# Attention values and turned probabilities as two float32r parts each: three products in place of one float32 product

## The chip, the cores and the metric

The kernel runs on one core of one Trainium2 chip, in one launch. The metric is the device time of the launch in microseconds (us), the median over the runs shown. A profiled execution gives one trace, with its own time; the words for the engines are PE (TensorE, matrix products), PEld (its weight loads), DVE (VectorE), ACT (ScalarE), POOL (GpSimd) and SP (SyncE, which here issues the transfers of the weights).

## The reference, cut to what matters

Two layers over 256 tokens of width 1024. Each layer is half a SwiGLU block, a mixer, and half a SwiGLU block. The mixer of layer 0 is a convolution module, that of layer 1 is multi-head latent attention with 8 heads. Only the attention is touched here:

```python
def mla(h, positions, w_a, g_q, g_kv, w_uq, w_ukv, w_o):
    ...
    kv = jnp.einsum("bsc,chd->bshd", c_kv, w_ukv)
    k_nope, v = kv[..., :QK_NOPE], kv[..., QK_NOPE:]
    ...
    for blk in range(seq // Q_BLOCK):
        q0, q1 = blk * Q_BLOCK, (blk + 1) * Q_BLOCK
        s = (q_nope . k_nope + q_rope . k_rope) * scale
        s = jnp.where(mask[None, None], s, -jnp.inf)
        p = jax.nn.softmax(s, axis=-1).astype(v.dtype)
        outs.append(jnp.einsum("bhqk,bkhd->bqhd", p, v[:, :q1]))
    o = jnp.concatenate(outs, axis=1)
    return o.reshape(o.shape[0], seq, N_HEADS * V_HEAD) @ w_o
```

(the two products of `s` are written short here). Blocks of 128 queries see 128 and 256 keys, so that a head has three 128 by 128 tiles of probabilities.

## The kernel before, in words

**Weights.** Every weight comes from memory as a float32 block of 1 MB (`raw`, three buffers, issued by SP). `load` (L161) splits it into two float32r parts: ACT copies it to `hi` (L187), which rounds it, and DVE subtracts to get `lo` (L188); both in two pieces of 128x1024. There are five buffers of `hi` and `lo`. `casts` keeps the two instructions of each piece, so that later code can place them. A product of two such split operands is `mm3` (L271): three matmuls, high times low (L273), high times high (L276) and low times high (L277).

**Placing.** A scheduler lays out each engine's order from the program's order, priorities and a simulated timeline. `urgent` (L193) gives a function's instructions high priority and remembers the last one on each engine; `behind` puts the two casts of a later block after the last six remembered ones on their engine. `order(a, b)` puts `a` after `b` on one engine without a semaphore. Each engine then runs its own instructions strictly in the order laid out.

**PSUM.** Eight banks in three groups (`bank`): four of "A" (products), three of "B" (scores and turned tiles), one of "C" (here: the values of a head, `pv`).

**The attention stage**, from `mla_in`: queries and keys are made per head (`nope`, L1240 copies them out), and the values `VV` are made for all heads as four products of 512 columns, each copied from its bank by ACT (L1287). Then, for each head:

1. `scores`: float32 products of queries and keys into a bank "B" (L1299, L1300).
2. `softmax`, urgent: DVE takes the maxima (L1312) and scales them (L1313), ACT takes the powers and their sums (L1315), DVE the reciprocal (L1318) and the scaling (L1320), into `pr`.
3. `probs`: PE turns the three tiles of `pr` into a bank "B" (L317), and ACT copies them to `ptT` in float32 (L1327).
4. `values`: two float32 products into the one bank "C", 256 columns with the first 128 keys (L1336) and 128 columns with the second (L1337).
5. `evicted`: ACT casts the bank to `Oh` (L1331) and DVE subtracts to `Ol` (L1332). The next head's `values` can write the bank when both have read it. This is urgent for heads 3 to 6 only.

The output product `o` (`Rows`, with the four blocks of `w_o`, here wo[0] to wo[3]) adds head after head in four banks "A", by `mm3`. The loop at the end of `mla_in` writes heads in a staggered order: `scores(i)`, `probs(i - 2)`, `values(i - 3)`, with blocks of `o` and further weight loads between. Ahead of it stand four manual placements of the `lo` casts of wo[0] and wo[1] behind steps of the softmax of heads 0 to 2.

Of the kernel before, what the change touches and what calls it, by code (L numbers as in the profile page):

```python
# [11 lines left out]
F32 = mybir.dt.float32  # L12
F32R = mybir.dt.float32r
# [6 lines left out]
P = 128  # L20
D = 1024
S = 256
NT = S // P
# [8 lines left out]
H = 8  # L32
NOPE = 128
ROPE = 64
VH = 128
# [49 lines left out]
def trunk(ctx: ExitStack, tc: tile.TileContext, x, xt, first, pos, invf, gfin, wdw,  # L85
          f1w13, f1w2, f2w13, f2w2, cw1, cw2, wa, wuq, wukv, wo, wpair, out):
    nc = tc.nc
# [12 lines left out]
    def uid(s):  # L100
        n_uid[0] += 1
        return f"{s}_{n_uid[0]}"
# [4 lines left out]
    def bank(tag, name):  # L107
        return ps.tile([P, 512], F32, tag=tag, name=uid(name), bufs=BANKS[tag])
# [24 lines left out]
    n_used = [0]  # L133
# [3 lines left out]
    def order(ins, first):  # L137
        tc.add_manual_dep(ins.ins, first.name, mybir.DependencyInfo(
            mybir.DependencyClass.NoSync, mybir.DependencyReason.DATA), reason="order")
# [7 lines left out]
    casts = {}  # L147
# [45 lines left out]
    def urgent(f):  # L193

        def g(*args, **kw):
            traced = nc.cur_bb.bb.instructions
            n = len(traced)
            with tc.high_priority():
                r = f(*args, **kw)
            last = {ins.engine: ins for ins in traced[n:]}  # L200
            for engine, ins in last.items():
                ahead_of.setdefault(engine, []).append(ins)
            return r
        return g

    def load_ahead(ahead=W_BUFS - 2):
        load_to(min(len(blocks), n_used[0] + ahead))

    def load_to(last):
        while len(loaded) < last:  # L210
            loaded.append(load(blocks[len(loaded)], PIECES))

    def weights(n=1, more=True):
        out = []
        for _ in range(n):
            n_used[0] += 1
            if more:
                load_ahead()
            else:
                load_ahead(0)  # L220
            out.append(loaded[n_used[0] - 1])
        return out
# [19 lines left out]
    for k in range(KT):  # L242
        c = slice(k % 4 * 512, k % 4 * 512 + 512)
# [27 lines left out]
    def mm3(o, ah, al, bh, bl, start, stop, after=()):  # L271

        mm = nc.tensor.matmul(o, ah, bl, start=start, stop=False)  # L273
        for a in after:
            order(mm, a.ins)
        nc.tensor.matmul(o, ah, bh, start=False, stop=False)  # L276
        return nc.tensor.matmul(o, al, bh, start=False, stop=stop)  # L277
# [8 lines left out]
    def tbs(tb):  # L286
        return slice(tb * P, (tb + 1) * P)
# [26 lines left out]
    def transposed(src, q, n, after=(), turned=None):  # L314
        b = bank("B", "tp")
        for j in range(n):
            tp = nc.tensor.transpose(b[:, j * P:(j + 1) * P], src[:, (q + j) * P:(q + j + 1) * P], ident)  # L317
            if turned is not None:
                turned.append(tp)
            for a in after:  # L320
                order(tp, a.ins)
        return b
# [815 lines left out]
    def mla(X, make_next, cc, sn):  # L1138
        with tc.tile_pool(name="mla", bufs=1) as act:
            return mla_in(act, X, make_next, cc, sn)  # L1140

    def mla_in(act, X, make_next, cc, sn):
# [9 lines left out]
        for x, fill in ((KR, -1e30), (QR, 1.0)):  # L1152
            nc.gpsimd.memset(x, 0.0)
            for parity in range(2):
                for tb in range(NT):
                    row = 64 * (1 - parity) + 32 * tb
                    t = tb * P + (CHUNK if x is KR else 0)
# [67 lines left out]

        KN = xp.tile([P, H, S], F32, tag="Xh", name="KN")
        QN = xp.tile([P, H, S], F32, tag="Xl", name="QN")
        VV = act.tile([P, NT, H * VH], F32, tag="VV", name="VV")

        def nope(part, dst, nk, ch, cl, width, h0, heads, after=()):  # L1230

# [13 lines left out]
        qr, qu, lows, turned = [], [], [], []  # L1245
# [22 lines left out]
        for t in range(NT):  # L1268
            b = transposed(kd[t], 0, 1, (last,))
# [3 lines left out]
        for tb in range(NT):  # L1273
            b = transposed(qr[tb], 0, 4, (last,)).rearrange("p (j t) -> p j t", t=P)
# [6 lines left out]
        for tb in range(NT):  # L1281
            for d in range(2):
                b = bank("A", "v")
                for k in range(2):
                    c = slice(k * D + d * 512, k * D + d * 512 + 512)
                    mm3(b, CKh[:, k, tbs(tb)], CKl[:, k, tbs(tb)], hi[:, c], lo[:, c], k == 0, k == 1)
                kept = nc.scalar.copy(VV[:, tb, d * 512:(d + 1) * 512], b)  # L1287

        Oh = act.tile([P, H, S], F32R, tag="Oh", name="Oh")
        Ol = act.tile([P, H, S], F32R, tag="CQ", name="Ol")  # L1290

        score_last, maxima, powers, scaled = [], [], [], []

        def scores(hd):
            b = bank("B", "sc")
            sc = {0: b[:, :P], 1: b[:, P:P + S]}
            for qb in range(NT):
                n = (qb + 1) * P
                nc.tensor.matmul(sc[qb], QN[:, hd, tbs(qb)], KN[:, hd, :n], start=True, stop=False)  # L1299
                last = nc.tensor.matmul(sc[qb], QR[:, hd % 2, hd // 2, tbs(qb)], KR[:, hd % 2, :n], start=False,  # L1300
                                        stop=True)
            score_last.append(last)
            return softmax(sc)
# [19 lines left out]

        def probs(pr):
            b = transposed(pr, 0, 3)
            pt = act.tile([P, 3 * P], F32, tag="ptT", name=uid("ptT"), bufs=2)
            nc.scalar.copy(pt, b[:, :3 * P])  # L1327
            return pt

        def evicted(hd, b):  # L1330
            nc.scalar.copy(Oh[:, hd, :], b[:, :S])  # L1331
# [1 line left out]

        def values(hd, pt):
            b = bank("C", "pv")
            nc.tensor.matmul(b[:, :S], VV[:, 0, hd * VH:(hd + 1) * VH], pt[:, :S], start=True, stop=False)  # L1336
            nc.tensor.matmul(b[:, P:S], VV[:, 1, hd * VH:(hd + 1) * VH], pt[:, S:], start=False, stop=True)  # L1337

            (urgent if hd in (3, 4, 5, 6) else lambda f: f)(evicted)(hd, b)

        pr, pt = {}, {}
        part, = weights(1, False)
        load_ahead(1)

        table = urgent(nc.scalar.activation)(small.tile([P, 1], F32, tag="silu", name="exp"), neghalf, AF.Exp)
        order(table, kept.ins)
# [1 line left out]
        pr[1] = scores(1)  # L1348
        pr[2] = scores(2)

        for j, i, highs, lows in ((0, 0, None, maxima[2]), (0, 1, None, scaled[0]), (1, 0, powers[2], scaled[1]),
                                  (1, 1, powers[2], scaled[2])):
            for cast, first in zip(casts[n_used[0] + j, i], (highs, lows)):
                if first is not None:
                    order(cast, first.ins)
        nope(part, QN, 4, CQh, CQl, 512, 4, (0, 4), score_last[-1:])
        o = Rows(Oh, Ol, H)
        for i in range(2, H + 3):
            if 2 < i < H:
                pr[i] = scores(i)  # L1360
            if i == 6:
                load_ahead(5)
            if i in (3, 4):
                load_ahead(i - 1 + (i == 4))
            if i - 2 < H:
                pt[i - 2] = probs(pr[i - 2])
            if i - 3 in pt:
                values(i - 3, pt[i - 3])
            if i in (6, 8):
                o.block((i - 6) // 2)  # L1370

            if i in (8, 9):
                load_to(n_used[0] + i - 4)
# [39 lines left out]
    rows = ctx.enter_context(tc.tile_pool(name="rows", bufs=1))  # L1413
# [101 lines left out]
```

## Time and profile before

| | us |
|---|---|
| median of 3 runs | 919.18 |
| lowest and highest run | 918.69, 919.48 |
| the profiled execution, its own time | 918.68 |
| span of its trace | 916.9 |

The profiled execution lies 0.50 us below the median; 1.8 us of its time lie outside the span. Of the span, the attention stage from the making of the values to the last product of `w_o` that waits for a head takes the stretch from about 677 to 727 us. In the timeline view a row is one instruction, or several in succession by the same line on the same tiles: its start in us from the span's start, the time to the end of the last one, engine, line, operation, output and inputs, shape, and how many. A pair in square brackets is idle time of the engine before it, with what ended it. The ends of PE rows are modelled, since matmuls are pipelined: what one costs in a stream is read from start to start.

### The profile page before, as it was taken

The numbers are of one execution on the slowest core, as the hardware profiler recorded it, in microseconds if no ns is written. First come the engines' busy times: TensorE is split into PE (matmuls) and PEld (weight loads), VectorE is DVE, ScalarE is ACT, GpSimd is POOL, SyncE is SP. The second block draws the span as 40 slices with busy tenths as digits, with TensorE's granted clock in tenths as the row PEclk, the third lists the DMA queues.
The fourth block names the chain that finished last, engine by engine and source line by source line (L and its number), as shares of the span: only waits on it lengthen the run. The fifth ranks groups of instructions, "written<-read, shape, count | busy, mean of one in ns | idle before, by whom it ended". The sixth has DMA issues, their size and how long they took to land.

```text
span 916.9 us, 12085 instructions
## 1 busy us (share of the span) xinstructions
PE 908.9 (99%) x4337; PEld 764.6 (83%) x4337; DVE 591.1 (64%) x931; ACT 492.8 (54%) x842; POOL 127.6 (14%) x261
## 2 busy tenths in 40 slices
PE   9999999999999999999999999999999999999997
PEld 7888888898988888888888888888898888888886
DVE  6886764489987666655476665545768676566533
ACT  7654454388877444543364544443677574454422
POOL 1720000079951000000010000001400000000000
PEclk9999999999999999999999999999999999999999
DMA  9987776533227667766567777754445478776711
GB/s 339 321 294 248 277 253 222 188 139 138 93 85 270 243 233 239 251 222 226 184 203 271 260 244 239 239 203 132 168 143 184 149 258 277 250 250 217 252 46 46
DMA packets 65292, 194.73 MB, mean 212 GB/s; under 512 B 11728, under 2 KB 37200, under 8 KB 45904
## 3 DMA queue, kind: packets, MB, share of 16 engines
q1 hardware_dynamic: 64800, 193.28, 60.7%
q8 instruction: 34, 0.56, 0.2%
q10 hardware_dynamic: 432, 0.69, 0.2%
q14 instruction: 26, 0.21, 0.1%
HBM read 179.78 MB, written 14.16 MB: 212 GB/s over the span
## 4 chain that ended last, share of the span: by engine, by line
PE 99%; DMA 0%; ACT 0%; POOLq 0%; DVE 0%; issue 0%; POOL 0%; ACTq 0%
PE u L277 17%; PE u L273 17%; PE u L276 17%; PE o L273 10%; PE o L277 10%; PE o L276 10%; PE u L753 3%; PE gate L753 3%; PE o L988 2%; PE tp L317 1%; PE u L282 1%; PE pairs L796 1%; PE a L273 1%; PE a L277 1%; PE a L276 1%; PE nope L277 1%
## 5 line engine op out<-in xcount | busy, mean ns | idle before, releaser
L188 DVE TENSOR_TENSOR lo<-raw,hi 128x1024 fp32r<-128x1024 f32 (+1 forms) x292 | 344.8, 1220 | 175.9 <-ACT hi L187 174.8
L187 ACT CAST hi<-raw 128x1024 fp32r<-128x1024 f32 x294 | 292.6, 1047 | 240.8 <-PE o L277 85.5
L273 PE MATMUL u<-lo,Xh 128*128 128x512 f32 x688 | 268.0, 389 | 0.0
L276 PE MATMUL u<-hi,Xh 128*128 128x512 f32 x688 | 267.7, 389 | 0.0
L277 PE MATMUL u<-hi,Xl 128*128 128x512 f32 x688 | 267.6, 389 | 0.0
L277 PEld LDWEIGHTS u<-hi,Xl 128*128 128x128 f32 x688 | 129.1, 188 | 27.2 <-DVE Xl L336 0.5
L273 PEld LDWEIGHTS u<-lo,Xh 128*128 128x128 f32 x688 | 129.1, 188 | 27.0 <-DVE lo L188 0.4
L276 PEld LDWEIGHTS u<-hi,Xh 128*128 128x128 f32 x688 | 129.1, 188 | 27.0
L276 PE MATMUL o<-hi,Gh 128*128 128x512 f32 (+1 forms) x356 | 137.9, 387 | 0.0
L277 PE MATMUL o<-hi,Gl 128*128 128x512 f32 (+1 forms) x356 | 137.8, 387 | 0.0
L273 PE MATMUL o<-lo,Gh 128*128 128x512 f32 (+1 forms) x356 | 137.2, 387 | 0.0
L308 POOL TENSOR_TENSOR ms<-ss 128x1 f32<-128x1 f32 x16 | 10.0, 628 | 586.7 <-ACT junk L300 586.7
L277 PEld LDWEIGHTS o<-hi,Gl 128*128 128x128 f32 x356 | 66.9, 188 | 13.5
L273 PEld LDWEIGHTS o<-lo,Gh 128*128 128x128 f32 x356 | 66.9, 188 | 13.5
L276 PEld LDWEIGHTS o<-hi,Gh 128*128 128x128 f32 x356 | 66.9, 188 | 13.4
L640 DVE TENSOR_TENSOR Gl<-gb,Gh 128x512 fp32r<-128x512 f32 (+1 forms) x48 | 31.3, 652 | 56.6 <-ACT Gh L639 56.6
L639 ACT CAST Gh<-gb 128x512 fp32r<-128x512 f32 (+1 forms) x48 | 28.0, 583 | 73.3 <-DMA gb<-gd 73.3
L842 DVE SCALAR_TENSOR_TENSOR acc<-V,dw,acc 128x128 f32<-128x128 f32 (+1 forms) x174 | 53.9, 394 | 0.0
L863 ACT ACTIVATE prod<-V,dw 128x128 f32<-128x128 f32 (+1 forms) x128 | 45.6, 415 | 1.9 <-POOL Y L864 1.0
L715 DVE TENSOR_TENSOR s<-s,u 128x512 f32<-128x512 f32 (+1 forms) x48 | 30.5, 635 | 7.6 <-PE u L277 7.3
L714 ACT ACTIVATE s<-u,R 128x512 f32<-128x512 f32 (+1 forms) x48 | 31.2, 649 | 5.9 <-PE u L277 4.8
L864 POOL TENSOR_TENSOR odd<-odd,prod 128x128 f32<-128x128 f32 (+1 forms) x62 | 33.0, 536 | 0.2
(218 smaller groups left out, 858.1 us busy)
## 6 DMA issues: line engine op xcount, KB each, us to landing
raw<-in_f2w SPq DMA_DIRECT2D x66, 1024.0 KB, 4.9
raw<-in_f1w SPq DMA_DIRECT2D x62, 1024.0 KB, 5.0
raw<-in_cw SPq DMA_DIRECT2D x12, 1024.0 KB, 4.8
gd<-gt SPq DMA_DIRECT2D x160, 64.0 KB, 3.3
gb<-gd SPq DMA_DIRECT2D x40, 256.0 KB, 4.9
raw<-in_wo SPq DMA_DIRECT2D x4, 1024.0 KB, 4.8
raw<-in_wuq SPq DMA_DIRECT2D x3, 1024.0 KB, 4.8
raw<-in_f1w SPq DMA_DIRECT2D x8, 256.0 KB, 4.9
```

The source lines that it names most:

```text
L187: casts[len(loaded), i] = (nc.scalar.copy(hi[:, c], raw[:, c]), low.tensor_sub(lo[:, c], raw[:, c], hi[:, c].bitcast(F32)))
L188: low.tensor_sub(lo[:, c], raw[:, c], hi[:, c].bitcast(F32)))
L273: mm = nc.tensor.matmul(o, ah, bl, start=start, stop=False)
L276: nc.tensor.matmul(o, ah, bh, start=False, stop=False)
L277: return nc.tensor.matmul(o, al, bh, start=False, stop=stop)
L640: nc.vector.tensor_sub(Gl[:, f, tbs(tb)].rearrange("p t (i q) -> p t i q", q=32), bv, gh.bitcast(F32))
L714: nc.scalar.activation(s[:, :w], u[0, tb][:, :w], AF.Silu, scale=X.r[tb])
L715: nc.vector.tensor_mul(s[:, :w], s[:, :w], u[0, tb][:, w:] if both else u[1, tb])
L753: mm = nc.tensor.matmul(u[:, t], w[:, c], X.x[:, k, t], start=(k == 0), stop=(k == KT - 1))
L842: dve_last.append(nc.vector.scalar_tensor_tensor(out if j == j1 - 1 else y, v, w, y, op0=ALU.mult, op1=ALU.add))
L863: prods_last.append(nc.scalar.activation(p, v, AF.Copy, scale=w))
L864: pool_last.append(nc.gpsimd.tensor_tensor(o, o, p, op=ALU.add))
```

## The change

Values and turned probabilities become float32r pairs, and each of the two float32 products of a head becomes three float32r ones by `mm3`. That takes a second part of each operand, made by a subtraction on DVE: four `VL` of 128x512 for the values, and one `ptL` of 128x384 for each head. `VL` uses the buffers "hb" and "ht" of a pool that serves the normalisations on either side of the attention, `ptL` the three buffers "rp512" of the rotary step. Both subtractions are urgent. The two placements of wo[1]'s `lo` casts behind the softmax of heads 1 and 2 go; instead, they are put behind the `ptL` subtractions of heads 1 and 2.

```diff
-        VV = act.tile([P, NT, H * VH], F32, tag="VV", name="VV")
+
+        VV = act.tile([P, NT, H * VH], F32R, tag="VV", name="VV")
+        VL = {}
...
-                kept = nc.scalar.copy(VV[:, tb, d * 512:(d + 1) * 512], b)
+                vh = VV[:, tb, d * 512:(d + 1) * 512]
+                kept = nc.scalar.copy(vh, b)
+                VL[tb, d] = rows.tile([P, 512], F32R, tag=("hb", "ht")[d], name=uid("VL"), bufs=2)
+                urgent(nc.vector.tensor_sub)(VL[tb, d], b, vh.bitcast(F32))
...
+        turned_low = []
...
-            pt = act.tile([P, 3 * P], F32, tag="ptT", name=uid("ptT"), bufs=2)
+            pt = act.tile([P, 3 * P], F32R, tag="ptT", name=uid("ptT"), bufs=2)
             nc.scalar.copy(pt, b[:, :3 * P])
-            return pt
+            pl = act.tile([P, 512], F32R, tag="rp512", name=uid("ptL"), bufs=3)
+            turned_low.append(urgent(nc.vector.tensor_sub)(pl[:, :3 * P], b[:, :3 * P], pt.bitcast(F32)))
+            return pt, pl
...
-            nc.tensor.matmul(b[:, :S], VV[:, 0, hd * VH:(hd + 1) * VH], pt[:, :S], start=True, stop=False)
-            nc.tensor.matmul(b[:, P:S], VV[:, 1, hd * VH:(hd + 1) * VH], pt[:, S:], start=False, stop=True)
+            ph, pl = pt
+            c = slice(hd % 4 * VH, hd % 4 * VH + VH)
+            for tb, o, t in ((0, b[:, :S], slice(0, S)), (1, b[:, P:S], slice(S, S + P))):
+                mm3(o, VV[:, tb, hd * VH:(hd + 1) * VH], VL[tb, hd // 4][:, c], ph[:, t], pl[:, t], tb == 0, tb == 1)
...
+        n_part = n_used[0]
...
-        for j, i, highs, lows in ((0, 0, None, maxima[2]), (0, 1, None, scaled[0]), (1, 0, powers[2], scaled[1]),
-                                  (1, 1, powers[2], scaled[2])):
+        for j, i, highs, lows in ((0, 0, None, maxima[2]), (0, 1, None, scaled[0]), (1, 0, powers[2], None),
+                                  (1, 1, powers[2], None)):
...
                 pt[i - 2] = probs(pr[i - 2])
+                if i in (3, 4):
+                    order(casts[n_part + 1, i - 3][1], turned_low[-1].ins)
```

## The prediction

> **What bounds the kernel now.** I read the page first: its head, the granted clock, and the chain of work that ended last.
>
> ```profile
> span 916.9 us, 12085 instructions
> ...
> PE 908.9 (99%) x4337; PEld 764.6 (83%) x4337; DVE 591.1 (64%) x931; ACT 492.8 (54%) x842; POOL 127.6 (14%) x261
> ...
> PEclk9999999999999999999999999999999999999999
> ...
> PE 99%; DMA 0%; ACT 0%; POOLq 0%; DVE 0%; issue 0%; POOL 0%; ACTq 0%
> ```
>
> PE is the chain: 99% of it, with nine tenths of the full clock or more in every slice. So each ns of PE work in the attention stage is a ns of the end, in both directions, and a wait of PE that does not exist today is added whole. The second view is the list of PE's waits over the whole span.
>
> ```profile
> PE warm L265 <- DVE still L260: 1.0, 1, 1.0
> PE u L282 <- ACT Xh L457: 0.4, 1, 0.4
> ```
>
> Both belong to the start of the kernel. The trace has no wait of PE in the attention stage that a better order could give back, save a hint of 0.1 us that I come to below. A gain can therefore come only from cheaper products.
>
> **The products of a head.** The third view is PE's timeline where a head's values stand between long products of the output, and, for the price of split products, two neighbours in the queries' stage.
>
> ```profile
> 718.00 0.39 PE L276 MATMUL o<-hi,Oh 128*128 128x512 f32 x1
> 718.23 0.59 PE L1336 MATMUL pv<-ptT,VV 128*128 128x256 f32 x2
> 718.66 0.38 PE L1337 MATMUL pv<-ptT,VV 128*128 128x128 f32 x2
> 718.80 1.17 PE L277 MATMUL o<-hi,Ol 128*128 128x512 f32 x4
> 719.80 0.39 PE L273 MATMUL o<-lo,Oh 128*128 128x512 f32 x1
> ```
>
> ```profile
> 692.16 0.28 PE L276 MATMUL nope<-CQ,hi 128*128 128x256 f32 x1
> 692.28 0.28 PE L277 MATMUL nope<-CQ,lo 128*128 128x256 f32 x1
> ```
>
> A float32 product is two instructions. A 512-column split product takes 0.23 us from start to start (718.00 to 718.23). From 718.23 to 719.80 there are 1.57 us; four split products are 0.92 of it, so a head's values cost 0.65: 0.43 for 256 columns (718.23 to 718.66), and 0.22 for 128, that is 0.11 for each instruction. A split product of 256 columns takes 0.12 (692.16 to 692.28).
>
> After the change a head has three split products of 256 columns, 3 x 0.12 = 0.36, against 0.43: a gain of 0.07. The other three have 128 columns. No split product in the trace is that narrow, so I bound it. Below: 512 columns take 0.23 and 256 take 0.12, so by columns alone 128 would take some 0.07 (half of the difference of 0.11 comes off 0.12). Above: as if it ran at float32's rate, both instructions for one product, 0.22. Between them lies the row that I hold nearest, since it shows what an instruction costs when columns hardly count: the convolution's sums of squares, with one column.
>
> ```profile
> 248.59 1.17 PE L880 MATMUL ms<-ones,sq 128*128 128x1 f32 x10
> 249.63 0.47 PE L753 MATMUL u<-Xp,raw 128*128 128x128 f32 x2
> ```
>
> Ten of them take 1.04 us, 0.104 each, with a weight load of 128 columns before each. A narrow product cannot outrun its own weight load, and every one of the three products loads its own weights. I take 0.11, which is also what the 128-column float32 instruction takes.
>
> The Trainium skill, "TensorE: Matmul & The Clock Gate", section "LDWEIGHTS (loading the stationary operand)", gives a weight load's time as its columns over 1.2, which is 107 ns for 128 columns; the ten rows agree with it at 104 ns. It speaks against the change: at 107 ns three narrow products come to 0.32 us, a loss of 0.10 on the narrow half.
>
> So a head costs 0.36 + 0.33 = 0.69 in place of 0.65: +0.04, and **+0.35 us** for eight (0.044 before rounding). By the lower bound it is 0.36 + 0.21 = 0.57, -0.08 a head, -0.6 in all; by the upper one 0.36 + 0.66 = 1.02, +0.37 a head, +3.0 in all.
>
> **The added subtractions.** Twelve on DVE. Their prices are by subtractions and products that read a bank, and the rows below also give the copies on ACT that become casts.
>
> ```profile
> L1332 DVE TENSOR_TENSOR Ol<-pv,Oh x8: 416/425/426, 696.0 to 726.3; 128x256 fp32r<-128x256 f32 x8
> L715 DVE TENSOR_TENSOR s<-s,u 128x512 f32<-128x512 f32 (+1 forms) x48 | 30.5, 635 | 7.6 <-PE u L277 7.3
> L639 ACT CAST Gh<-gb 128x512 fp32r<-128x512 f32 (+1 forms) x48 | 28.0, 583 | 73.3 <-DMA gb<-gd 73.3
> L1287 ACT COPY VV<-v x4: 581/586/587, 678.7 to 684.3; 128x512 f32<-128x512 f32 x4
> ```
>
> A cast of 128x512 (583 ns) costs ACT what the copy does (586), so the high parts are free. A `VL` of 512 columns takes 0.64, a `ptL` of 384, halfway between 256 and 512, 0.53. In all 4 x 0.64 + 8 x 0.53 = 6.8 us of DVE.
>
> The four `VL` fall between 679 and 685.5, behind the copies of L1287, where DVE has next to nothing to do; I cost them at nothing. What hides them is the queries' products, which keep PE busy to 692.7 while the first softmax runs. The bank of a value product comes free 0.64 later, which the next user of the last one, the output product after the values of head 0, does not feel. With that cover gone, the last `VL` would hold back the first maxima by some 0.1. The buffers "hb", "ht" and "rp512" have had their last readers well before, and their next writers come after the last head: nothing.
>
> The eight `ptL` are another matter. In `mm3` the first product is high times low, so none of a head's six products can start before its `ptL`, and the turned tile's bank is held that much longer. Here is DVE from the first head's turning on, and ACT beside it.
>
> ```profile
> 691.79 2.35 DVE L188 TENSOR_TENSOR lo<-raw,hi 128x1024 fp32r<-128x1024 f32 x2
> 694.60 0.62 DVE L1312 TENSOR_REDUCE nm<-sc 128x1 f32<-128x128 f32 x2 [0.46 <-PE sc L1300]
> ...
> 695.99 0.42 DVE L1332 TENSOR_TENSOR Ol<-pv,Oh 128x256 fp32r<-128x256 f32 x1 [0.56 <-ACT Oh L1331]
> 696.80 0.17 DVE L1318 RECIPROCAL sm<-sm 128x2 f32<-128x2 f32 x1 [0.39 <-ACT pr L1315]
> ...
> 699.03 0.17 DVE L1318 RECIPROCAL sm<-sm 128x2 f32<-128x2 f32 x1 [0.98 <-ACT pr L1315]
> ...
> 699.97 2.36 DVE L188 TENSOR_TENSOR lo<-raw,hi 128x1024 fp32r<-128x1024 f32 x2 [0.18 <-ACT hi L187]
> 702.25 0.61 DVE L1312 TENSOR_REDUCE nm<-sc 128x1 f32<-128x128 f32 x2
> 702.78 2.35 DVE L188 TENSOR_TENSOR lo<-raw,hi 128x1024 fp32r<-128x1024 f32 x2
> 705.05 0.16 DVE L1313 TENSOR_SCALAR nm<-nm 128x2 f32<-128x2 f32 x1
> 705.12 0.42 DVE L1332 TENSOR_TENSOR Ol<-pv,Oh 128x256 fp32r<-128x256 f32 x1
> ...
> 706.39 0.55 DVE L1320 TENSOR_SCALAR pr<-pr,sm 128x128 f32<-128x128 f32 x2
> ```
>
> ```profile
> 693.44 0.48 ACT L1327 COPY ptT<-tp 128x384 f32<-128x384 f32 x1
> ...
> 698.89 3.88 ACT L187 CAST hi<-raw 128x1024 fp32r<-128x1024 f32 x4
> 702.67 0.37 ACT L1331 CAST Oh<-pv 128x256 fp32r<-128x256 f32 x1
> ```
>
> ```profile
> 694.73 0.60 PE L1336 MATMUL pv<-ptT,VV 128*128 128x256 f32 x2
> ...
> 705.59 0.70 PE L1336 MATMUL pv<-ptT,VV 128*128 128x256 f32 x2
> ...
> 707.27 0.38 PE L1299 MATMUL sc<-KN,QN 128*128 128x128 f32 x2
> ...
> 708.58 0.49 PE L317 MATMUL tp<-ident,pr 128*128 128x128 f32 x3
> ```
>
> Head 0: its turned tile is copied at 693.92, and its values start at 694.73. The two casts of 691.79 (wo[1]) are moved away, so DVE is free; the subtraction ends at 694.45. Cost nothing, with 0.28 to spare.
>
> **The place that decides is 705.** Bank "C" is single: the values of head 2 start at 705.59, just when `Ol` of head 1 has ended (705.12 + 0.42 = 705.54), and the pair takes 0.70 instead of the 0.59 of 718.23, the hint of 0.1 named above. So here PE already runs with no slack on DVE, which is busy from 699.97 without a break: `Ol` of head 1, not urgent, stands behind four casts (wo[2] and wo[3]). Now count what is put ahead of it. The casts of wo[1], 2.35, move from before 694.14 to after the `ptL` of heads 1 and 2; and the `ptL` of heads 1, 2 and 3 are added, 1.6. Together 3.95 us, into a stretch whose idle pieces are 0.46 + 0.56 + 0.39 + 0.98 + 0.18 = 2.57. Each piece is shorter than one cast (half of 2.35), so a cast that begins in one pushes the softmax steps behind it, and these push the next powers on ACT; I let half of the idle time be used, 1.3. `Ol` of head 1 is then late by 3.95 - 1.3 = 2.65 (bounds: 1.4 with all of it used, 3.95 with none; and 0 if the casts of wo[2] and wo[3] are laid out behind `Ol`). Behind the waiting products stand all of PE's later ones. In the new order PE can have the scores of head 7 ahead of them: four pairs of instructions, 2 x 0.22 + 2 x 0.43 = 1.3 by the prices above, of which I count 0.85, since their bank waits for a `ptL` too. That leaves **+1.8 us** of wait (from 0 to 3.95). What is late next: the maxima of head 5, hence its scaling (706.39 to 706.94) and its turning at 708.58. That has 1.6 us of room, and 3.4 when PE is itself 1.8 late, against the 2.65; I add nothing.
>
> Last, the transfers.
>
> ```profile
> raw<-in_f2w SPq DMA_DIRECT2D x66, 1024.0 KB, 4.9
> ```
>
> ```profile
> L179 SPq DMA_DIRECT2D raw<-in_f2w x3: 327/327/328, 694.2 to 705.2; - x3
> ...
> 707.52 2.01 ACT L187 CAST hi<-raw 128x1024 fp32r<-128x1024 f32 x2
> ```
>
> SP issues the next block at 694.2, when the last cast of wo[1] ends; with those casts near 700 it is issued some 6 us later and lands 4.9 later, near 705, before its own cast at 707.52. Nothing, with 2.5 us of room; that block feeds the feed-forward stage after 727.
>
> **The sum** against the profiled execution: 918.68 + 0.35 + 1.8 = 920.83, and since that execution lies 0.50 below the median, **921.3 us** in the median.
>
> **The rivals.**
>
> *The order absorbs it.* The scheduler sees the new subtractions and lays out the casts of wo[2] and wo[3] behind `Ol`, or more of PE's work ahead of the values of head 2. For it: wo[2] and wo[3] hold the weights of heads 4 to 7, which the output needs last, so nothing but their place in the program puts them first. Against it: the casts stand ahead of that `Ol` in the program, and did so in this trace although the bank was wanted. Then only the products remain: 919.18 + 0.35 = 919.5, no measurable change (I take 0.2%, 1.84 us, as what a measurement of this kernel can tell). It decides from the point where `Ol` of head 1 starts no later than the products that wait for it.
>
> *The narrow product goes by columns.* At 0.07 it gives -0.6, and the 0.1 at 705 may go as well: 918.5 with no wait. For it: the steps of 512 and 256 columns lie on a line. Against: the ten one-column rows. The Trainium skill's section "Back-to-back issue gap" of the same page gives 81 ns for 128 columns in a stream of loads and matmuls; by that a head would be 0.60 and the change -0.4; the nearest rows, 104 ns, do not bear it out.
>
> *The narrow product falls back to float32's rate,* so that the split doesn't do what it says for a third of the columns: +3.0, 922.2 alone and 924.0 with the wait. For it: nothing but that no split product narrower than 256 columns is in the trace, and that this kernel's 128-column products all take two instructions.
>
> **How the numbers follow.** The forecast has 0.46 (its own range, 920.6 to 923.5, by a wait between 1.1 and 3.95); 0.06 of that lies within 0.2%. The order that absorbs it 0.24, all within 0.2%. Narrow by columns 0.12, of which 0.06 goes to faster by over 0.2%, for a gain that the rows leave no room for but that new placing of the whole stage could bring. The fall back 0.18, all slower. That makes slower 0.40 + 0.18 = 0.58, within 0.2% 0.06 + 0.24 + 0.06 = 0.36, faster 0.06. The range goes from the rival by columns, 918.5, to the fall back with its wait and a little more, 924.5.
>
> **What would show it.** Right: narrow products 0.11 from start to start; a gap in PE before the values of head 2, ended by `Ol`, with the casts of wo[1] to wo[3] ahead of it on DVE. Wrong: narrow products at 0.07 or 0.22; `Ol` of head 1 before those casts; a wait of PE for a `ptL` or for a bank of "B", which I cost at nothing; or any change outside 677 to 727 us.

## The result and the profile after

| | before | after |
|---|---|---|
| median, 7 runs each, us | 918.74 | 921.6 |
| lowest and highest | 918.28, 919.48 | 921.46, 922.54 |
| the profiled execution | 918.68 | 922.09 |
| its span | 916.9 | 920.3 |

The changed kernel is slower by 2.86 us; the ratio is 1.0033, with a 95% interval from 1.0023 to 1.0043 (2.1 to 4.0 us). The forecast was 921.3, a change of 2.15 from the 919.18 of the first three runs. In the experiments below the kernel before ran again beside each group, with medians from 918.94 to 919.06; differences are taken against the one of the same group.

The page after, the same lines as before:

```profile
span 920.3 us, 12130 instructions
...
PE 910.6 (99%) x4353; PEld 765.7 (83%) x4353; DVE 596.7 (65%) x943; ACT 492.4 (54%) x842; POOL 127.4 (14%) x261
...
PE 94%; DMA 2%; DVE 2%; ACT 1%; SPq 0%; issue 0%; POOLq 0%; POOL 0%; DVEq 0%; ACTq 0%
```

PE is no longer all of the chain. The 2% of DMA belong to transfers awaited before 15 us and between 120 and 131 us, far ahead of the attention. PE's list of waits names the new one; after the name stand the total, the number of times and the longest, in us:

```profile
PE o L273 <- ACT Oh L1339: 1.6, 1, 1.6
...
PE o L273 <- DVE s L715: 0.2, 1, 0.2
PE u L273 <- DVE lo L188: 0.2, 1, 0.2
```

The first is in the attention stage. The last two are in the first feed-forward stage, at 131.86 and 17.11 us. Up to 674 us the two traces hold the same instructions in the same order on each of PE, ACT, DVE, POOL and SP. By the first product of the values, still ahead of the first changed instruction of PE, this execution is already 0.91 us later than the one of before (677.96 in the timeline after, 677.05 before):

```profile
677.96 0.48 PE L273 MATMUL v<-lo,CKh 128*128 128x512 f32 x1
```

```profile
677.05 0.48 PE L273 MATMUL v<-lo,CKh 128*128 128x512 f32 x1
```

So 0.9 of the 3.4 us between the two profiled executions is not the change's, and times of the two timelines are compared below with 0.91 taken off. The first product behind the attention, before and after, gives a second mark:

```profile
730.15 0.48 PE L273 MATMUL u<-lo,Xh 128*128 128x512 f32 x1
```

```profile
733.55 0.48 PE L273 MATMUL u<-lo,Xh 128*128 128x512 f32 x1
```

From the one mark to the other the stage takes 53.10 us before (677.05 to 730.15) and 55.59 after (677.96 to 733.55): 2.49 more. What follows takes 186.7 us in both. This length leaves out what differs ahead of the stage. It comes from one execution of each kernel; the one kernel that was profiled twice (experiment 9) gave 52.45 and 52.44. The experiments below give it beside the medians, as "stage", against the 53.10 of before.

**The products.** PE's timeline after, one head between long output products:

```profile
713.68 0.39 PE L276 MATMUL o<-hi,Oh 128*128 128x512 f32 x1
713.91 0.28 PE L273 MATMUL pv<-ptL,VV 128*128 128x256 f32 x1
714.03 0.28 PE L276 MATMUL pv<-ptT,VV 128*128 128x256 f32 x1
714.14 0.28 PE L277 MATMUL pv<-ptT,VL 128*128 128x256 f32 x1
714.26 0.23 PE L273 MATMUL pv<-ptL,VV 128*128 128x128 f32 x1
714.33 0.27 PE L276 MATMUL pv<-ptT,VV 128*128 128x128 f32 x1
714.43 0.27 PE L277 MATMUL pv<-ptT,VL 128*128 128x128 f32 x1
714.55 1.14 PE L277 MATMUL o<-hi,Ol 128*128 128x512 f32 x4
715.53 0.49 PE L317 MATMUL tp<-ident,pr 128*128 128x128 f32 x3
```

From 713.91 to 715.53 there are 1.62 us with four output products, against 1.57 before: a head's values cost 0.70 (1.62 less the 0.92 of four output products), 0.05 more. Eight heads make 0.4.

**The wait.** PE, ACT and DVE after, at the place where the stage stops:

```profile
703.94 0.59 PE L1306 MATMUL sc<-KR,QR 128*128 128x256 f32 x2
706.14 0.50 PE L273 MATMUL o<-lo,Oh 128*128 128x512 f32 x1 [1.61 <-ACT Oh L1339]
...
708.09 0.49 PE L317 MATMUL tp<-ident,pr 128*128 128x128 f32 x3
708.73 0.36 PE L273 MATMUL pv<-ptL,VV 128*128 128x256 f32 x1
```

```profile
701.13 0.37 ACT L1321 ACTIVATE pr<-sc,nm 128x128 f32<-128x128 f32 x1 [2.43 <-DVE nm L1319]
...
701.94 3.88 ACT L187 CAST hi<-raw 128x1024 fp32r<-128x1024 f32 x4
705.72 0.37 ACT L1339 CAST Oh<-pv 128x256 fp32r<-128x256 f32 x1
```

```profile
696.35 0.56 DVE L199 TENSOR_TENSOR ptL<-tp,ptT 128x384 fp32r<-128x384 f32 x1
696.82 1.22 DVE L188 TENSOR_TENSOR lo<-raw,hi 128x1024 fp32r<-128x1024 f32 x1
...
699.33 0.56 DVE L199 TENSOR_TENSOR ptL<-tp,ptT 128x384 fp32r<-128x384 f32 x1
699.80 1.22 DVE L188 TENSOR_TENSOR lo<-raw,hi 128x1024 fp32r<-128x1024 f32 x1
700.93 0.17 DVE L1319 TENSOR_SCALAR nm<-nm 128x2 f32<-128x2 f32 x1
...
705.83 2.35 DVE L188 TENSOR_TENSOR lo<-raw,hi 128x1024 fp32r<-128x1024 f32 x2
...
708.17 0.42 DVE L1340 TENSOR_TENSOR Ol<-pv,Oh 128x256 fp32r<-128x256 f32 x1
```

The row of before that answers to 700.93 is this:

```profile
697.89 0.16 DVE L1313 TENSOR_SCALAR nm<-nm 128x2 f32<-128x2 f32 x1
```

Read backwards from PE. After the last scores at 703.94 (two instructions of 0.215) PE could go on at 704.37; it goes on at 706.14, 1.77 later, when ACT has cast `Oh` of head 1. ACT does that at 705.72, behind four casts of wo[2] and wo[3] (701.94); these stand behind the powers of head 4, which ACT has waited for, 2.43 us idle, until DVE gave it their scaled maxima at 700.93. DVE is late because the `ptL` of heads 1 and 2 and the two casts of wo[1] stand ahead. Before, that instruction ran at 697.89: it is 3.04 later, 2.1 of it the change's. A smaller wait follows at the values of head 2: the turning at 708.09 is done by 708.42 (3 x 0.11), `Ol` of head 1 ends at 708.59, and the products start at 708.73, 0.31 late. Together 2.1 us, 2.0 more than the 0.1 of before; with the products' 0.4 that makes 2.4 of the 2.49 by which the stage is longer.

The two waits have one cause, and the second one sets the end. From the products at 708.73 the chain of work that ended last goes back to `Ol` on DVE, not to `Oh`:

```profile
701.13 0.91 ACT pr L1321 x4
702.05 0.95 ACT hi L187
703.02 1.59 DVE lo L188 x2
...
708.26 0.33 DVE Ol L1340
708.73 0.36 PE pv L273
```

A row gives the start, the time, the engine and what it does. The late powers on ACT make its casts late, 701.94 (701.03 with 0.91 taken off) against 698.89, and DVE's casts of wo[2] and wo[3] wait for those; `Ol` of head 1 stands behind them. Without the 1.77 for `Oh` PE would have been ready for the values of head 2 at 706.65 (708.42 less 1.77) and would have waited there until 708.73 all the same. That is worked out from the rows; no run moved `Oh` alone.

### The profile page after: what moved, and what is told of

Read it like the earlier page. It is cut to its first block, busy times and chain, and to the rows that moved or that the text cites. A ratio compares the mean times of both kernels' runs of the same rounds, so it can differ in the third digit from the quotient of the medians.

```text
span 920.3 us, 12130 instructions
## 1 busy us (share of the span) xinstructions
PE 910.6 (99%) x4353; PEld 765.7 (83%) x4353; DVE 596.7 (65%) x943; ACT 492.4 (54%) x842; POOL 127.4 (14%) x261
## 4 chain that ended last, share of the span: by engine, by line
PE 94%; DMA 2%; DVE 2%; ACT 1%; SPq 0%; issue 0%; POOLq 0%; POOL 0%; DVEq 0%; ACTq 0%
PE u L277 17%; PE u L273 17%; PE u L276 17%; PE o L277 9%; PE o L273 9%; PE o L276 9%; PE u L753 3%; PE gate L753 3%; PE o L988 2%; DMA raw<-in_f1w 1%; PE tp L317 1%; DVE lo L188 1%; PE pairs L796 1%; PE a L277 1%; PE a L276 1%; PE a L273 1%
## 5 line engine op out<-in xcount | busy, mean ns | idle before, releaser
L349 DVE STREAM_TRANSPOSE gt<-s 128x512 f32<-128x512 f32 (+1 forms) x48 | 32.0, 667 | 1.4
```

The costliest lines, as they stand in the source:

```text
L349: nc.vector.transpose(t[:, :w], src.rearrange("p (t j q) -> p j t q", t=n, q=32))
```

## The experiments

Theory W: the loss is this wait, made by what is put ahead on DVE. The expectations speak of its longer piece, the one for `Oh`; by the chain above it is one delay with two ends. Rival P: the products themselves. Rival L: PE is held by the `ptL` that a head's first product reads.

**1. The products alone.** No subtraction is made, and the casts of wo[1] are placed as before. All three products of a pair read the high parts; the low parts are left out.

```diff
-                VL[tb, d] = rows.tile(...)
-                urgent(nc.vector.tensor_sub)(VL[tb, d], b, vh.bitcast(F32))
...
-            turned_low.append(urgent(nc.vector.tensor_sub)(pl[:, :3 * P], b[:, :3 * P], pt.bitcast(F32)))
-            return pt, pl
+            return pt, pt
...
-                mm3(o, VV[...], VL[tb, hd // 4][:, c], ph[:, t], pl[:, t], tb == 0, tb == 1)
+                mm3(o, VV[...], VV[...], ph[:, t], pl[:, t], tb == 0, tb == 1)
```

> The six split products of a head without the subtractions: all three products of a pair read the high parts, no VL and no ptL is made, and the casts of wo[1] keep their places of before; the low parts are left out of the values. Theory W (the loss is a wait that the new DVE work makes: the negated maxima of head 4 come late, with them the powers, the four casts of wo[2] and wo[3] on ACT and the cast Oh of head 1, which PE waits for): without that work only the products' own price is left, 0.05 us a head, so +0.4 us on the kernel before, 0.2 to 0.7, and no wait of PE at the output product of head 1. Rival P (the products themselves cost the 2.9 us, in the stretches that the trace does not show as waits): +2 to +3 us.

Measured: 919.13 against 918.94, +0.2; ratio 1.0003 (0.9994 to 1.0012); stage +0.32. PE has no wait in the stage. P falls.

**2. The subtractions and the placements alone.** The products are those of before, on the high parts; nothing reads the low parts.

```diff
-                mm3(o, VV[...], VL[tb, hd // 4][:, c], ph[:, t], pl[:, t], tb == 0, tb == 1)
+                nc.tensor.matmul(o, VV[...].bitcast(F32), ph[:, t].bitcast(F32), start=tb == 0, stop=tb == 1)
```

> The subtractions and the placements of the changed kernel, with the products of before (two float32 products a head, reading the high parts; nothing reads VL and ptL, and the low parts are left out of the values). Theory W: the wait stays, +1.8 to +2.4 us on the kernel before, and 0.4 less than the changed kernel; in the trace PE waits some 1.6 us for Oh of head 1. Rival P: within 0.5 us of the kernel before. Rival L (PE is held by the ptL that its first product reads): the wait goes, since no product reads them, within 0.5 us of the kernel before.

Measured: 921.4, +2.5; ratio 1.0029 (1.0017 to 1.0041); stage +2.22. The wait stands as in the changed kernel, in PE's list:

```profile
PE o L273 <- ACT Oh L1339: 1.7, 1, 1.7
```

No product reads a `ptL` here, so L falls with P. The two halves, 0.2 and 2.5, make 2.7 of the 2.86; by the stages 0.32 and 2.22 make 2.54, against 2.49 for the whole.

**3. The casts of wo[1] back in their place.**

```diff
-        ..., (1, 0, powers[2], None), (1, 1, powers[2], None)):
+        ..., (1, 0, powers[2], scaled[1]), (1, 1, powers[2], scaled[2])):
...
-                if i in (3, 4):
-                    order(casts[n_part + 1, i - 3][1], turned_low[-1].ins)
```

> The changed kernel with the casts of wo[1] back behind the softmax of heads 1 and 2, as before. Theory W, with the moved casts as its main part: the maxima of head 4 are then late by the subtractions of heads 0 to 2 only, less than 1 us in place of 2; head 0's subtraction comes behind the casts, near 695, and its products wait some 0.3 us. In all +0.6 to +1.6 us on the kernel before, a gain of 1.3 to 2.3 on the changed one. Rival (the subtractions alone fill DVE, and the place of the casts does not matter): within 0.5 us of the changed kernel.

Measured: 919.63, +0.7; ratio 1.0009 (1.0000 to 1.0018); stage +0.89. The wait for `Oh` is gone; what is left is the other one, at the values of head 2:

```profile
PE pv L273 <- DVE Ol L1340: 0.4, 1, 0.4
```

All the subtractions are still there. So putting two casts back takes some 2 us off the 2.86, and 1.60 off the stage. The wait of 0.3 us that I expected at the products of head 0 is not in PE's list.

**4. Those casts moved in the kernel before,** with nothing else changed. They go behind the maxima and the scaling of head 3, about where the changed kernel has them.

```diff
+            if i == 3:
+                order(casts[n_part + 1, 0][1], maxima[3].ins)
+                order(casts[n_part + 1, 1][1], scaled[3].ins)
```

> The kernel before, with float32 products and no subtraction added, in which only the casts of wo[1] are moved: behind the maxima and the scaling of head 3, about where the changed kernel has them. Theory W, with the moved casts as its main part: they alone make the maxima of head 4 late by 1 to 2 us, and PE waits 0.8 to 1.6 us for Oh of head 1: +0.8 to +1.8 us on the kernel before. Rival (casts and subtractions are late only together, since the idle pieces of DVE hold either): within 0.4 us of the kernel before.

Measured: 920.25 against 918.95, +1.3; ratio 1.0015 (1.0006 to 1.0024); stage +1.45. The size is as expected, but the wait is at another place than I wrote. PE's list, then DVE and ACT:

```profile
PE tp L317 <- ACT pr L1315: 1.3, 1, 1.3
```

```profile
697.76 1.21 DVE L188 TENSOR_TENSOR lo<-raw,hi 128x1024 fp32r<-128x1024 f32 x1
...
699.23 0.16 DVE L1313 TENSOR_SCALAR nm<-nm 128x2 f32<-128x2 f32 x1
```

```profile
699.42 0.37 ACT L1315 ACTIVATE pr<-sc,nm 128x128 f32<-128x128 f32 x1 [1.58 <-DVE nm L1313]
...
700.23 3.88 ACT L187 CAST hi<-raw 128x1024 fp32r<-128x1024 f32 x4
704.00 0.37 ACT L1315 ACTIVATE pr<-sc,nm 128x128 f32<-128x128 f32 x1
```

The scaled maxima of head 4 come behind the second cast, at 699.23, ACT idles for them, and the four casts follow. Here the scheduler has put the powers of head 5 (704.00) next behind those casts, and a turning of PE waits for the bank "B" that they read. It is the same cause, late maxima of head 4 ahead of four casts on ACT, with another instruction at its end.

**5. The eviction of heads 1 and 2 urgent.**

```diff
-            (urgent if hd in (3, 4, 5, 6) else lambda f: f)(evicted)(hd, b)
+            (urgent if hd in (1, 2, 3, 4, 5, 6) else lambda f: f)(evicted)(hd, b)
```

> The changed kernel with the eviction of heads 1 and 2 urgent too, as it is for heads 3 to 6, so that the cast Oh of head 1 may be laid out ahead of the four casts of wo[2] and wo[3] on ACT. Theory W: PE's wait for Oh of head 1 goes or falls below 0.5 us; +0.3 to +1.0 us on the kernel before. Rival P: no gain on the changed kernel, +2.4 to +3.2.

Measured: 921.23, +2.3; ratio 1.0026 (1.0016 to 1.0037); stage +2.47, with the wait for `Oh` at 1.6 as in the changed kernel. That is near the number that I gave to rival P, but the run decides nothing: on ACT the four casts still stood ahead of `Oh` of head 1. The priority did not move that cast. My guess is that its turn, in the scheduler's timeline, comes when the casts are already laid out; no run shows that.

**6. The order written out,** so that the cast is moved for certain.

```diff
+                out_of = values(i - 3, pt[i - 3])
+                if i == 4:
+                    for piece in range(PIECES):
+                        for cast, first in zip(casts[n_part + 3, piece], out_of):
+                            order(cast, first.ins)
```

(`values` and `evicted` return the eviction's two instructions here, so that `Oh` on ACT and `Ol` on DVE both go ahead of the casts of wo[3].)

> The changed kernel with an order written out: the high casts of wo[3] behind the cast Oh of head 1 on ACT, its low casts behind Ol of head 1 on DVE. (The urgent flag of the run e4_urgent did not move that cast.) Theory W: Oh of head 1 comes 1.9 us earlier, after two casts in place of four, so that PE's wait of 1.6 us at the output product falls to zero or little, and the wait for Ol at the values of head 2 goes too: +0.4 to +1.0 us on the kernel before. Rival (the wait at head 1 is only where a general lateness of the stage shows, and it turns up again at a later head): +1.8 us or more.

Measured: 919.34 against 918.95, +0.4; ratio 1.0004 (0.9995 to 1.0013); stage +0.50. ACT now has `Oh` between the casts, DVE has `Ol` between its own, and the wait for `Oh` is gone from PE's list, although ACT's idle time for the maxima is the same 2.43 as in the changed kernel:

```profile
700.23 0.37 ACT L1321 ACTIVATE pr<-sc,nm 128x128 f32<-128x128 f32 x1 [2.43 <-DVE nm L1319]
...
701.04 1.99 ACT L187 CAST hi<-raw 128x1024 fp32r<-128x1024 f32 x2
702.92 0.38 ACT L1339 CAST Oh<-pv 128x256 fp32r<-128x256 f32 x1
703.18 2.01 ACT L187 CAST hi<-raw 128x1024 fp32r<-128x1024 f32 x2
```

```profile
704.93 0.41 DVE L1340 TENSOR_TENSOR Ol<-pv,Oh 128x256 fp32r<-128x256 f32 x1
```

So late maxima do harm only through the casts that are queued behind them, on ACT and with these on DVE, ahead of `Oh` and `Ol`. The edit moves both, so it doesn't tell them apart. Of the 0.50 the products are 0.32; the rest is 0.17 of waiting at the values of head 2, which start at 705.49.

**7. Both: the old place and the written order.** Edits 3 and 6 together.

> The changed kernel with both: the casts of wo[1] in their old place, and the written order of Oh and Ol of head 1 ahead of wo[3]'s casts. Theory W: no wait of PE is left in the stage, so only the products' price remains: +0.2 to +0.6 us on the kernel before, and 0.2 to 0.5 less than the run e3_oldplace.

Measured: 919.07, +0.1; ratio 1.0000 (0.9991 to 1.0009); stage +0.25; PE's list has no wait in the stage. The full split, with its twelve subtractions, can be had at no price that could be measured, but at no gain.

**8. The price of a narrow product by itself.** Edit 1, with the three products of 128 columns issued three times over:

```diff
-                mm3(o, VV[...], VV[...], ph[:, t], pl[:, t], tb == 0, tb == 1)
+                for n in range(1 if tb == 0 else 3):
+                    mm3(o, VV[...], VV[...], ph[:, t], pl[:, t], tb == 0, tb == 1 and n == 2)
```

> As e1_products, with the three products of 128 columns issued three times over: six more narrow split products a head, 48 in all, that read the high parts again (the second keys' part of the values is counted threefold). It measures the disputed price by itself. At 0.11 each, the weight load's pace: +5.3 us on e1_products, so +5.5 on the kernel before. By columns, 0.07: +3.4 and +3.6. At float32's rate, 0.22: +10.6.

Measured: 924.2 against 919.06, +5.1; ratio 1.0055 (1.0042 to 1.0069); stage +5.51. Less the 0.2 of experiment 1, the 48 added products cost 4.95 us, 0.103 each, to some 0.03 either way by the two intervals. By the stages, 5.51 less 0.32, they cost 5.19 us, 0.108 each. PE's timeline has the same pace:

```profile
701.54 0.28 PE L273 MATMUL pv<-ptT,VV 128*128 128x128 f32 x1
701.65 0.27 PE L276 MATMUL pv<-ptT,VV 128*128 128x128 f32 x1
701.77 0.27 PE L277 MATMUL pv<-ptT,VV 128*128 128x128 f32 x1
```

**9. Split products for the 256 columns alone.** Edit 7, with the second keys' values (`VF`) and the last turned tile (`pf`) in float32.

```diff
-            for tb, o, t in ((0, b[:, :S], slice(0, S)), (1, b[:, P:S], slice(S, S + P))):
-                mm3(o, VV[...], VL[tb, hd // 4][:, c], ph[:, t], pl[:, t], tb == 0, tb == 1)
+            mm3(b[:, :S], VV[:, hd * VH:(hd + 1) * VH], VL[hd // 4][:, c], ph, pl[:, :S], True, False)
+            nc.tensor.matmul(b[:, P:S], VF[:, hd * VH:(hd + 1) * VH], pf, start=False, stop=True)
```

> As e10_old_order, but split products for the 256 columns alone; the 128 columns stay one float32 product, with the second keys' values and the last turned tile kept in float32. By the rows a head then costs 0.36 + 0.22 = 0.58 in place of 0.65: -0.07 a head, -0.6 us in all, and the 0.1 of wait in the kernel before goes: -0.3 to -0.8 us on the kernel before. If narrow products were cheap (0.07), it would be no better than e10_old_order; with the price of 0.11 it is 0.9 us better than that.

Measured: 918.4, -0.55; ratio 0.9995 (0.9986 to 1.0004); stage -0.65. By the medians it is not told apart from the kernel before. It was run again beside the written order alone (edit 6 in the kernel before):

> The kernel before, float32 products, with only the written order of Oh and Ol of head 1 ahead of wo[3]'s casts. It tells how much of the gain of e8_mixed is the order's. Theory W: the order has no more than the 0.1 us of wait at the values of head 2 to give, so -0.3 to +0.2 us on the kernel before. Rival (e8_mixed is faster by the order, not by cheaper products): -0.4 to -0.8.

> The kernel of e8_mixed once more, beside the run with the order alone: -0.3 to -0.8 us on the kernel before by cheaper 256-column products; within 0.2 us of e11_before_order if the order made the gain.

Measured: the order alone 918.83 against 919.06, -0.2, ratio 0.9997 (0.9989 to 1.0005), stage -0.06; the mixed kernel 918.36, -0.7, ratio 0.9991 (0.9983 to 0.9999), stage -0.66. The second interval ends just below 1, and both runs have the expected size. By the stages some 0.6 of it is not the order's. PE's timeline of the first run shows where it comes from:

```profile
714.45 0.28 PE L273 MATMUL pv<-ptL,VV 128*128 128x256 f32 x1
...
714.80 0.39 PE L1351 MATMUL pv<-ptF,VF 128*128 128x128 f32 x2
714.94 1.17 PE L277 MATMUL o<-hi,Ol 128*128 128x512 f32 x4
715.95 0.27 PE L317 MATMUL tp<-ident,pr 128*128 128x128 f32 x1
```

From 714.45 to 715.95 there are 1.50 us, so a head costs 0.58, against 0.65 before and 0.70 after; for eight heads that is 0.56 less than before. It is the fastest of all the kernels here, by a gain of less than 0.1%.

## Why the prediction was right, and where it was not

- **PE as the bound, and nothing to give back:** right. The stage of before had no wait worth having: the written order alone gives 0.2, within its interval's reach of nothing, and 0.06 in the stage.
- **The products, +0.35:** right. 0.4 by the timeline, 0.32 in the stage and 0.2 in the median of the run of the products alone. The term that was bounded from 0.07 to 0.22, the narrow product, was taken as 0.11 and measured as 0.103 by the medians and 0.108 by the stages. The Trainium skill's rule for weight loads ("TensorE: Matmul & The Clock Gate", section "LDWEIGHTS (loading the stationary operand)"), 107 ns for 128 columns, agrees with these 108 ns. The 81 ns of its section "Back-to-back issue gap" does not: by an estimate from it the 48 products would cost 3.9 us, in place of the 5.19 measured in the stage.
- **The `VL` at nothing, head 0's `ptL` at nothing, the longer hold of bank "B" at nothing:** right for the changed kernel, as far as no wait of PE for any of them is in its list, and the run without readers of `ptL` is no faster than by the products. The late transfer at nothing: right too; SP issues it at 701.1 instead of 694.2, and PE has no wait behind 706.14 in its list.
- **The wait, +1.8:** right in size (2.0), in the cause (the casts of wo[1] and the subtractions ahead on DVE) and in what sets its end. The step read "The place that decides is 705", the values of head 2, by `Ol` of head 1 on DVE, and there the chain goes. It did not have the wait for `Oh` on ACT, ahead of that place, in which PE spends 1.77 of it. And it had the way wrong by which the delay reaches `Ol`. I followed it along DVE's own queue and counted idle pieces there; I did not follow it through the scaled maxima of head 4 to the four casts behind them on ACT, for which DVE's own casts wait, though the rows for it were shown: four casts from 698.89, and `Oh` of head 1 only at 702.67.
- **Luck in the size:** `Ol` of head 1 came 2.14 late (708.17 less 0.91, against 705.12), not 2.65. The 0.85 taken off for the scores of head 7 was not had; PE has these only at 710.42, behind the values of head 2. One error made the wait too long and the other too short, so that 1.8 came this near to 2.0 is in part luck. So is 921.3 beside 921.6: the forecast started from 919.18, the median of three runs, and that of seven is 918.74. As changes, 2.15 stands against 2.86 by the medians and 2.49 in the stage.
- **Which part of it:** the prediction did not divide the wait. The runs do, by the stages: with the casts in their old place 0.89 are lost, 0.57 beyond the products; the moved casts alone make 1.45; both together 2.22. So the casts are the larger part. That the two together make 0.2 more than their sum rests on one execution of each; by the medians (0.5, 1.3 and 2.5) it is within the intervals, of 0.8 to 1.1 us to either side.
- **The rivals:** the order that absorbs it did not come about by itself, but written out by hand it does what that rival said: +0.4 and +0.1 by the medians, 0.50 and 0.25 in the stage, where the products alone make 0.32. The prices by columns (0.07) and at float32's rate (0.22) are both ruled out by the run with nine narrow products a head (0.108).

What stays open is some 0.4 us between the 2.49 of the stage and the 2.86 between the medians. In the traces nothing behind the stage differs, and what differs ahead of it differs between the same instructions. It is less than the interval's half width, and no run was made for it.

## What to carry to other kernels

Before a float32 product is split into three, look at its width: here 256 columns gain 0.07 us a head (0.36 against 0.43), and 128 columns lose 0.12 (0.34 against 0.22), since a product of 128 columns took 0.11 and one of 256 only 0.12. When work is added to an engine with idle time, the idle time is not the measure; follow the first late instruction to the engine that waits for it, then along what is queued there, and on to whoever waits for that. A wait that is long need not be the one that sets the end; the chain of work that ended last tells which does. When a change is smaller than what executions differ by, compare the stage that it touches, between marks in the traces, beside the medians. A long weight cast ahead of a short eviction can be worth an explicit order: here a priority alone left it where it was.

## What the runs showed of the hardware that was not expected

The first narrow product behind a wide one starts the next after 0.07 us (714.26 to 714.33), below the pace of 0.11 at which the rest follow. It looks as if its weights had been loaded under the wide product, but no run was made to tell this from the way in which the starts are recorded. Nothing is saved by it over a head: from end to end it costs 0.70, of which three products of 256 columns are 0.36, so that the three narrow ones come to 0.34, 0.11 each.
